# A decoder block's first stage: two shift/scale columns made earlier, output weights cut between the attention pairs, two heads of a pair interleaved

## The chip, the cores and the metric

The kernel runs on one core of one Trainium2 chip. The time is device microseconds from launch to end; before the change it is 1597.16 us, the median of three runs (1595.16 to 1599.23). A profiled execution of the same program took 1595.99 us; the span in its trace, from the first to the last instruction, is 1594.3 us.

## The reference, cut to what matters

One token block of 512 rows and 1024 columns goes through two sub-layers. The change is in the first: six vectors are made from the condition `c`, the rows are modulated, projected, sent through two kinds of attention, and the result is normalised per group and multiplied by an output matrix.

```python
ada = einsum('bd,de->be', silu(c), w_ada) + b_ada
shift1, scale1, gate1, shift2, scale2, gate2 = split(ada, 6)
h = x * (1.0 + scale1) + shift1
qa, ka, va, qb, kb, vb = split(h @ w_in)
# oa: 8 heads of 64 in a window of 128 keys, distance bias and a sink logit
#   (two key heads; query head j and j+4 share the pair number j)
scores = q @ k / sqrt(64) + bias           # blocks of 128 queries x 256 keys
m = max(max(scores), sink);  p = exp(scores - m)
oa = (p / (sum(p) + exp(sink - m))) @ va
# ob: 8 heads of 64, stick-breaking weights over all earlier keys
ob = stick_breaking(qb, kb, vb)
mix = concat(rms_norm(oa), rms_norm(ob)) @ w_out
x = layer_norm(ALPHA * x + gate1 * mix)
h = x * (1.0 + scale2) + shift2            # into the second sub-layer (PEER)
```

shift2 and scale2 are columns 3 and 4 of the six; gate1 is number 2. They are first needed when the first sub-layer is done.

## The kernel before, in words

The program is one core's work on five engines. TensorE (PE) multiplies, VectorE (DVE), ScalarE (ACT) and GpSimd (POOL) do the rest, SyncE (SP) issues the transfers. Each engine works off its list in order. In the first stage these lists are set by a scheduler that goes through the program text in its order, prefers parts marked `tc.high_priority()`, and fills in others as it thinks their inputs will be ready; tiles with the same tag share a ring of `bufs` buffers, and a step that needs a buffer waits for its last user. The later stages are written in a manual order and are not touched.

The first stage: the modulated rows are kept transposed, as a high and a low part (`hhi`, `hlo`). A projection chunk (`proj_chunk`, L303) loads 512 KB of weights into `uraw`, cuts them into `uhi` (ScalarE, L92) and `ulo` (VectorE, L93) and runs 24 matmuls of 512 columns into `pj`. `uraw`, `uhi` and `ulo` have two buffers each.

Stick-breaking works on pairs of heads j = 0 to 3. `sb_weights` takes the two heads one after the other through one score tile `z` (one buffer): scores `z<-q,k` (L367); ScalarE takes Abs, Exp and Ln into `e` (L370 to L372); VectorE makes the logarithms (L374); GpSimd masks them (L340, L342); two small VectorE steps (L376, L377); the cut into `sphi` (ScalarE) and `splo` (VectorE, L93); matmuls that add up the logarithms (L382, L384, first with `sphi`, then with `splo`); Exp into `e` (L387), masked again. `e` has two buffers, so the next pair's first head waits until `sb_values` (L398, `oacc<-e,vr`) has read the last pair's. Both functions are high priority.

Windowed attention works on pairs too (`swa_pair`, four of them). `swa_head` makes one head: eight score matmuls in the trace for one head (L421, `zs`, 64 of the 128 rows of the array, as each fp32 matmul is two records), a maximum with bias and sink (L424), exponentials (L431), the sum and the scaling by it (L436). Then `swa_pair` transposes the weights (`pt`, L451), copies them (L453, `pts`) and multiplies with the values (L456, `oacc`). `zs` and `pt` share the tag `s` with two PSUM banks; `oacc` of both kinds of attention is one bank.

The columns of shift2 and scale2 come from `ada_cols`: 4 MB of weights, eight VectorE steps into `acc` (L170, L172), eight matmuls with one column each (L179, `adap`), and one small addition (L181). The text has `ada_cols(3)` behind the projection chunks 6 and 7, and `ada_cols(4)` behind `sb_values` of pair 2. The output weights are eight slices: `load_wo` loads one into the same ring `uraw`, multiplies by gate1 (L502) and cuts it (`wohi`, `wolo`). Six of them follow the last projection chunk in the text, and the pair `swa_pair(3)` follows them. The output matmuls are `zm` (L556); the group norms need `ssp` (L521), a sum over all heads' squares.

```python
        w = sb(2, q0, k0)
        swa_pair(0, qa, ka)
        qa1 = proj_chunk(10, "qa")
        swa_pair(1, qa1, ka)
        q0, k0 = proj_chunk(6, "q"), proj_chunk(7, "k")
        ada_cols(3)
        sbv(2, w)
        ada_cols(4)
        w = sb(3, q0, k0)
```

Of the kernel before, what the change touches and what calls it, by code (L numbers as in the profile page):

```python
# [8 lines left out]
F32 = mybir.dt.float32  # L9
F32R = mybir.dt.float32r  # L10
# [4 lines left out]
AF = mybir.ActivationFunctionType  # L15
OP = mybir.AluOpType
# [16 lines left out]
NEG = -1e30  # L33
# [34 lines left out]
def tile_block(ctx, tc, xr, xT, ccol, wada, bcol, brow, wqk, wv, sinks, gncol, wout,  # L68
               ln1c, ln1r, wq, keys, u_rows, uT, v_rows, ln2r, out):
    nc = tc.nc  # L70
    V, A, G, T = nc.vector, nc.scalar, nc.gpsimd, nc.tensor
# [4 lines left out]
    wsp = ctx.enter_context(tc.tile_pool(name="wsp", bufs=2))  # L76
    small = ctx.enter_context(tc.tile_pool(name="small", bufs=2))
# [9 lines left out]
                    base=0, channel_multiplier=-1)  # L87
# [54 lines left out]
    with ExitStack() as front:  # L142
        fc = front.enter_context(tc.tile_pool(name="fc", bufs=1, side="right", reuse_waits="tile"))
        fa_cm = tc.tile_pool(name="fa", bufs=2, side="right")
        fa = fa_cm.__enter__()
        fw_cm = tc.tile_pool(name="fw", bufs=2)
        fw = fw_cm.__enter__()
        ps = front.enter_context(tc.tile_pool(name="psf", bufs=2, space=PSUM))
# [51 lines left out]
        part = fc.tile([P, 1], F32, name="part")  # L200
# [93 lines left out]
        def proj_chunk(i, nm):  # L294
            if i < 4:
                half_proj(i, len(PARTS) - 1)
                p = heads[i][1]
            else:
                hi, lo = load_w_in(i)
                p = ps.tile([P, S], F32, name="pj", tag="m", bufs=2)  # L300
                for dc in range(DC):
                    for n, (a, b) in enumerate(((hi, hhi), (hi, hlo), (lo, hhi))):
                        T.matmul(p, a[:, dc], b[:, dc], start=(dc == 0 and n == 0), stop=(dc == DC - 1 and n == 2))  # L303
            o = fw.tile([P, S], F32, name=nm, tag=nm)
            A.activation(o, p, AF.Copy, scale=0.125 if nm[0] == "q" else 1.0)
            return o

        vr = fw.tile([P, TB, 640], F32, name="vr", bufs=1)

        def proj_v(*halves):  # L310
            for half in halves:
# [5 lines left out]
                for tb in range(TB):  # L317
                    p = ps.tile([P, S], F32, name="pj", tag="m", bufs=2)
                    t = slice(tb * P, (tb + 1) * P)
                    for dc in range(DC):  # L320
# [11 lines left out]
                        base=0, channel_multiplier=1)  # L332
# [74 lines left out]
        def swa_head(j, r, qt, kt):  # L407
            h = j + 4 * r
            rs = slice(r * HD, (r + 1) * HD)
            prs = fw.tile([P, TB, 2 * P], F32, name="prs", bufs=3)  # L410
            nm, den, es = (small.tile([P, TB], F32, name=n, bufs=3) for n in ("nm", "den", "es"))
            bias = fw.tile([P, 2 * P], F32, name="bias")
            V.tensor_scalar(bias, dist, -(2.0 ** (-(h + 1.0))), None, op0=OP.mult)
            for keep_op, base, cm, st in ((OP.is_ge, P, 1, -1), (OP.is_gt, 0, -1, 1)):
                G.affine_select(out=bias, in_=bias, pattern=[[st, 2 * P]], compare_op=keep_op, fill=NEG,
                                base=base, channel_multiplier=cm)
            k0 = [P if qb == 0 else 0 for qb in range(TB)]
            for qh in range(2):
                z = ps.tile([P, 2, 2 * P], F32, name="zs", tag="s")
                for qb in (2 * qh, 2 * qh + 1):  # L420
                    T.matmul(z[:, qb % 2, k0[qb]:], qt[rs, qb * P:(qb + 1) * P],  # L421
                             kt[rs, (qb - 1) * P + k0[qb]:(qb + 1) * P], start=True, stop=True, skip_group_check=True)
                for qb in (2 * qh, 2 * qh + 1):
                    V.tensor_tensor_reduce(out=prs[:, qb, k0[qb]:], in0=z[:, qb % 2, k0[qb]:], in1=bias[:, k0[qb]:],  # L424
                                           scale=1.0, scalar=sink[:, h:h + 1], op0=OP.add, op1=OP.max,
                                           accum_out=nm[:, qb:qb + 1])
            V.tensor_scalar(nm, nm, -1.0, None, op0=OP.mult)
            V.tensor_scalar(es, nm, sink[:, h:h + 1], None, op0=OP.add)
            A.activation(es, es, AF.Exp)
            for qb in range(TB):  # L430
                A.activation(prs[:, qb, k0[qb]:], prs[:, qb, k0[qb]:], AF.Exp, bias=nm[:, qb:qb + 1],  # L431
                             accum_out=den[:, qb:qb + 1])
            V.tensor_tensor(den, den, es, op=OP.add)
            V.reciprocal(den, den)
            for qb in range(TB):
                V.tensor_scalar(prs[:, qb, k0[qb]:], prs[:, qb, k0[qb]:], den[:, qb:qb + 1], None, op0=OP.mult)  # L436
            return prs

        def swa_pair(j, qt, kt):
            prs = [swa_head(j, r, qt, kt) for r in range(2)]  # L440
            o = ps.tile([P, S], F32, name="oacc", tag="o", bufs=1)
            blocks = [(qb, kb) for qb in range(TB) for kb in ((qb - 1, qb) if qb else (qb,))]
            for n0 in (0, 4):
                part = blocks[n0:n0 + 4]
                w = len(part) * P
                pts = []
                for r in range(2):
                    pt = ps.tile([P, 512], F32, name="pt", tag="s")
# [48 lines left out]
        wo = [None] * DC

        def load_wo(c, pool):
            raw = wsp.tile([P, D], F32, name="uraw", tag="uraw")  # L500
            nc.sync.dma_start(raw, wout[c])
            V.tensor_tensor(raw, raw, gate1, op=OP.mult)  # L502
            wo[c] = (pool.tile([P, D], F32R, name=f"wohi{c}"), pool.tile([P, D], F32R, name=f"wolo{c}"))
            split(raw, *wo[c])

        ORDER = (4, 5, 6, 7, 0, 1, 2, 3)
# [670 lines left out]
```

## Time and profile before

| | |
|---|---|
| time, median of three runs | 1597.16 us |
| profiled execution, time and span | 1595.99 us, 1594.3 us |
| TensorE busy | 1554.9 us, 98% of the span |
| VectorE, ScalarE, GpSimd busy | 77%, 41%, 29% |
[...]
| the attention part of the first stage | about 58 to 257 us of the span |

[...] A timeline row gives the start in us from the span's start, how long the run of instructions took, engine, source line, operation, output and inputs, shape and count; in brackets how long the engine sat idle before it and what released it. A run that has no bracket began as soon as the one before it was done. The busy time of a pipelined TensorE contains overlap, so 98% does not mean that it works at its peak. The share of the whole span says little about one stage: the change is worth what it does between about 130 and 270 us.

### The profile page before, as it was taken

What the parts mean: (1) busy time and instruction counts of PE and PEld (TensorE: products, weight loads), DVE (VectorE), ACT (ScalarE), POOL (GpSimd) and SP (SyncE); (2) the same over time, 40 slices, a digit from 0 to 9 for tenths busy, and PEclk for the clock granted to TensorE, in tenths of its full rate; (3) what the DMA queues carried; (4) which work ended last, traced back from release to release, by engine and by line L of the source; (5) the groups of instructions that cost most, each with busy time, mean ns of one, the idle gap of its engine ahead of it and who ended that gap; (6) DMA issues with size and microseconds to landing.
All of it is one profiled execution on the core that took longest, in us unless ns stands there. A gap on an engine that the chain in (4) does not pass through costs nothing.

```text
span 1594.3 us, 21985 instructions
## 1 busy us (share of the span) xinstructions
PE 1554.9 (98%) x8109; PEld 1346.3 (84%) x8109; DVE 1220.3 (77%) x2351; ACT 647.5 (41%) x935; POOL 455.8 (29%) x410
## 2 busy tenths in 40 slices
PE   8999999999989999999999999999999999999996
PEld 5776767788879999899999999999999999998885
DVE  2568585589999997578777787777877777777878
ACT  2535574333355555333333333333333333333331
POOL 0002133544400000233334333333333444333100
PEclk8999898999999999999999999999999999999999
DMA  9564132222225555999888988999889998989873
GB/s 338 184 258 158 53 112 101 79 92 81 81 80 212 219 210 202 334 327 326 305 311 301 326 301 304 306 309 322 302 303 312 307 321 301 311 282 305 261 231 119
DMA packets 147356, 382.12 MB, mean 240 GB/s; under 512 B 11312, under 2 KB 68656, under 8 KB 143280
## 3 DMA queue, kind: packets, MB, share of 16 engines
q1 hardware_dynamic: 110384, 246.49, 44.6%
q0 software_dynamic: 36864, 134.23, 24.4%
q8 instruction: 63, 1.03, 0.3%
q14 instruction: 45, 0.37, 0.1%
HBM read 351.32 MB, written 29.36 MB: 239 GB/s over the span
## 4 chain that ended last, share of the span: by engine, by line
PE 79%; DVE 12%; DMA 3%; ACT 3%; issue 1%; POOL 1%; SPq 0%; DVEq 0%; ACTq 0%; POOLq 0%
PE yb L980 32%; PE ph L970 25%; PE pw L841 5%; PE ph L806 4%; PE pj L303 3%; PE zm L556 2%; DVE scr L620 1%; PE pj L274 1%; DMA wa<-in_wada_dram 1%; DVE tsi L622 1%; DVE tsi L619 1%; PE pq L647 1%; DVE tsv L621 1%; DVE tsv L618 1%; PE oacc L398 1%
## 5 line engine op out<-in xcount | busy, mean ns | idle before, releaser
L855 POOL DMA_INDIRECT gat<-in_u_rows_dram,idx x128 | 161.6, 1262 | 478.5 <-DVE hd L873 226.5
L93 DVE TENSOR_TENSOR ulo<-uraw,uhi 128x1024 fp32r<-128x1024 f32 x133 | 162.5, 1223 | 164.9 <-ACT uhi L92 160.5
L970 PE MATMUL ph<-h2hi,ulo 128*128 128x384 f32 x768 | 258.6, 337 | 0.6 <-DVE ulo L93 0.6
L970 PE MATMUL ph<-h2hi,uhi 128*128 128x384 f32 x768 | 258.2, 336 | 0.3 <-ACT uhi L92 0.3
L970 PE MATMUL ph<-h2lo,uhi 128*128 128x384 f32 x768 | 258.2, 336 | 0.0
L855 POOL DMA_INDIRECT gat<-in_v_rows_dram,idx x128 | 161.0, 1258 | 264.8 <-DVE y L883 224.1
L980 PE MATMUL yb<-vhi,ghi 128*128 128x512 f32 x654 | 203.0, 391 | 0.0
L980 PE MATMUL yb<-vhi,glo 128*128 128x512 f32 x654 | 202.9, 391 | 0.0
L980 PE MATMUL yb<-vlo,ghi 128*128 128x512 f32 x654 | 202.6, 391 | 0.0
L92 ACT ACTIVATE uhi<-uraw 128x1024 fp32r<-128x1024 f32 x155 | 162.4, 1050 | 74.6 <-PE pq L647 52.9
L883 DVE SCALAR_TENSOR_TENSOR y<-gat,cf,y 128x1024 f32<-128x1024 f32 x127 | 162.7, 1281 | 3.9 <-DMA gat<-in_v_rows_dram,idx 1.6
L873 DVE CUSTOM_DVE_ANT_0 gscr<-gat,h2row 128x1024 f32<-128x1024 f32 x128 | 156.5, 1222 | 10.6 <-DMA gat<-in_u_rows_dram,idx 7.9
L1085 ACT ACTIVATE stash<-ph 128x384 f32<-128x384 f32 x96 | 47.2, 491 | 275.1 <-PE ph L970 275.1
L970 PEld LDWEIGHTS ph<-h2lo,uhi 128*128 128x128 f32 x768 | 144.4, 188 | 4.4
L970 PEld LDWEIGHTS ph<-h2hi,uhi 128*128 128x128 f32 x768 | 144.4, 188 | 4.4 <-ACT uhi L92 0.7
L980 PEld LDWEIGHTS yb<-vlo,ghi 128*128 128x128 f32 x654 | 122.7, 188 | 27.3
L980 PEld LDWEIGHTS yb<-vhi,glo 128*128 128x128 f32 x654 | 122.8, 188 | 26.8
L970 PEld LDWEIGHTS ph<-h2hi,ulo 128*128 128x128 f32 x768 | 144.4, 188 | 1.0 <-DVE ulo L93 1.0
L980 PEld LDWEIGHTS yb<-vhi,ghi 128*128 128x128 f32 x654 | 121.8, 188 | 18.9
L93 DVE TENSOR_TENSOR vlo<-vraw,vhi 128x1024 fp32r<-128x1024 f32 x97 | 118.4, 1220 | 17.5 <-ACT vhi L92 17.4
L92 ACT ACTIVATE vhi<-vraw 128x1024 fp32r<-128x1024 f32 x97 | 102.8, 1060 | 53.6 <-issue 35.8
L947 ACT ACTIVATE ghi<-gt 128x384 fp32r<-128x384 f32 x97 | 51.0, 525 | 177.7 <-DVE gt L920 177.7
(311 smaller groups left out, 2860.1 us busy)
## 6 DMA issues: line engine op xcount, KB each, us to landing
uraw<-in_uT_dram SPq DMA_DIRECT2D x128, 512.0 KB, 5.2
vraw<-in_v_rows_dram SPq DMA_DIRECT2D x128, 512.0 KB, 5.2
w_d<-stage SPq DMA_DIRECT2D x12, 2048.0 KB, 7.3
wt<-w_d SPq DMA_DIRECT2D x32, 768.0 KB, 9.3
wa<-in_wada_dram SPq DMA_DIRECT2D x16, 1024.0 KB, 6.5
wah<-in_wada_dram SPq DMA_DIRECT2D x16, 512.0 KB, 9.4
uraw<-in_wq_dram SPq DMA_DIRECT2D x16, 512.0 KB, 3.3
uraw<-in_wqk_dram SPq DMA_DIRECT2D x11, 512.0 KB, 7.8
```

The costliest lines, as they stand in the source:

```text
L92: A.activation(hi, src, AF.Copy)
L93: (eng or V).tensor_tensor(lo, src, hi.bitcast(F32), op=OP.subtract)
L303: T.matmul(p, a[:, dc], b[:, dc], start=(dc == 0 and n == 0), stop=(dc == DC - 1 and n == 2))
L806: T.matmul(p[:, :ND], a[:, dc], b[:, dc, P:], start=(dc == 0 and n == 0), stop=(dc == DC - 1 and n == 2))
L841: T.matmul(p[:, k * P:(k + 1) * P], oh4[:, 1, :, k], oh4[:, 2 + j, :, k], start=(j == 0), stop=(j == 1), skip_group_check=True)
L855: G.indirect_dma_start(out=t, out_offset=None, in_=rows, in_offset=bass.IndirectOffsetOnAxis(ap=idx[:, k:k + 1], axis=0))
L873: V.tensor_tensor_reduce(out=scr, in0=t, in1=h2row, scale=1.0, scalar=0.0, op0=OP.mult, op1=OP.add, accum_out=hd[:, n:n + 1])
L883: V.scalar_tensor_tensor(y0, t, cf[:, k:k + 1], y0, op0=OP.mult, op1=OP.add)
L947: A.activation(gop[i][0], gts[i], AF.Copy)
L970: T.matmul(p[:, :ND], a[:, dc], b[:, dc, P:], start=(dc == 0 and n == 0), stop=(dc == DC - 1 and n == 2))
L980: T.matmul(ybank[b][c0 // 512][:, c0 % 512:(c1 - 1) % 512 + 1], x[:, t], y[:, c0:c1], start=(i == 0 and n == 0), stop=(n == 2 and i == (NK ...
L1085: A.activation(stash[i + LOOK], p[:, :ND], AF.Gelu_apprx_tanh)
```

## The change

Three edits in the first stage. `ada_cols(3)` and `ada_cols(4)`, and with them the release of the memory that their weights used, move ahead of `sb(2, ...)`. The six `load_wo` calls are spread over the text between the pairs. `swa_head` becomes `swa_scores`, which issues the score matmuls of both heads of a pair in turn, two score tiles at a time. In `swa_pair` the value matmuls are ordered by key block, so that two neighbouring query blocks go in one matmul of 256 columns: 8 for a pair where there were 14.

```diff
+        def swa_scores(j, qt, kt):
...
             for qh in range(2):
-                z = ps.tile([P, 2, 2 * P], F32, name="zs", tag="s")
+                zs = [ps.tile([P, 2, 2 * P], F32, name="zs", tag="s") for _ in range(2)]
                 for qb in (2 * qh, 2 * qh + 1):
-                    T.matmul(z[:, qb % 2, k0[qb]:], qt[rs, qb * P:(qb + 1) * P],
+                    for r in range(2):
+                        rs = slice(r * HD, (r + 1) * HD)
+                        T.matmul(zs[r][:, qb % 2, k0[qb]:], qt[rs, qb * P:(qb + 1) * P],
...
-            blocks = [(qb, kb) for qb in range(TB) for kb in ((qb - 1, qb) if qb else (qb,))]
+            blocks = [(qb, kb) for kb in range(TB) for qb in (kb, kb + 1) if qb < TB]
...
-                for n, (qb, kb) in enumerate(part):
+                for n in range(0, len(part), 2):
+                    qb, kb = part[n]
+                    c = min(2 * P, w - n * P)
...
         ka = proj_chunk(8, "ka")
+        ada_cols(3)
+        ada_cols(4)
+        fa_cm.__exit__(None, None, None)
+        fwo = front.enter_context(tc.tile_pool(name="fwo", bufs=1, side="right", reuse_waits="tile"))
         w = sb(2, q0, k0)
         swa_pair(0, qa, ka)
         qa1 = proj_chunk(10, "qa")
+        load_wo(ORDER[0], fwo)
         swa_pair(1, qa1, ka)
         q0, k0 = proj_chunk(6, "q"), proj_chunk(7, "k")
-        ada_cols(3)
+        load_wo(ORDER[1], fwo)
+        load_wo(ORDER[2], fwo)
         sbv(2, w)
-        ada_cols(4)
         w = sb(3, q0, k0)
...
         qa2 = proj_chunk(11, "qa")
+        load_wo(ORDER[3], fwo)
+        load_wo(ORDER[4], fwo)
+        load_wo(ORDER[5], fwo)
         swa_pair(2, qa2, ka)
         sbv(3, w)
         qa3 = proj_chunk(12, "qa")
...
-        for c in ORDER[:6]:
-            load_wo(c, fwo)
         swa_pair(3, qa3, ka)
```

Because a scheduler sets the lists, the text alone does not tell what stands where. Three places matter. The lines of the changed kernel are numbered anew: L421, L424, L436, L502 and L556 of before are L424, L430, L446, L488 and L573.

TensorE behind the last matmul of chunk 8 (`ka`), before; `zs` are the first pair's scores, `pj` is chunk 10, `z<-sphi` and `z<-splo` belong to the second head of stick-breaking pair 1:

```order
L421 MATMUL zs<-ka,qa 128x128
L421 MATMUL zs<-ka,qa 128x256 x3
L303 MATMUL pj<-hhi,ulo 128x512
L303 MATMUL pj<-hhi,uhi 128x512
L303 MATMUL pj<-hlo,uhi 128x512
L303 MATMUL pj<-hhi,ulo 128x512
L382 MATMUL z<-sphi,negtri 128x512 x2
L382 MATMUL z<-sphi,negtri 128x256
```

and now, from the same place to the second run of `adap`:

```order
L179 MATMUL adap<-ones,acc 128x1 x8
L424 MATMUL zs<-ka,qa 128x128 x2
L424 MATMUL zs<-ka,qa 128x256 x2
L382 MATMUL z<-sphi,negtri 128x512 x2
...
L382 MATMUL z<-splo,negtri 128x512 x2
L382 MATMUL z<-splo,negtri 128x256
L384 MATMUL z<-splo,negone 128x384
L384 MATMUL z<-splo,negone 128x256 x2
L384 MATMUL z<-splo,negone 128x128
L179 MATMUL adap<-ones,acc 128x1 x8
L303 MATMUL pj<-hhi,uhi 128x512
L303 MATMUL pj<-hlo,uhi 128x512
```

Both runs of `adap` stand here now, and the matmuls of chunk 10 stand behind the second of them.

VectorE at the same place, before, from the logarithms of that head (`e<-z,e`) to the low part `splo`:

```order
L374 SCALAR_TENSOR_TENSOR e<-z,e 128x1280
L93 TENSOR_TENSOR ulo<-uraw,uhi 128x1024
L376 COPY e<-e 128x128
L377 TENSOR_TENSOR e<-e 128x128
L93 TENSOR_TENSOR ulo<-uraw,uhi 128x1024
L424 ISA prs,nm<-zs,bias,sink 128x128
L424 ISA nm 128x1
L424 ISA prs,nm<-zs,bias,sink 128x256
L424 ISA nm 128x1
L93 TENSOR_TENSOR splo<-e,sphi 128x1536
```

and now:

```order
L374 SCALAR_TENSOR_TENSOR e<-z,e 128x1280
L181 TENSOR_TENSOR adac<-adap,bc 128x8
L172 SCALAR_TENSOR_TENSOR acc<-wa,silu,acc 128x1024
L376 COPY e<-e 128x128
L377 TENSOR_TENSOR e<-e 128x128
L172 SCALAR_TENSOR_TENSOR acc<-wa,silu,acc 128x1024
L430 ISA prs,nm<-zs,bias,sink 128x128
L430 ISA nm 128x1
L172 SCALAR_TENSOR_TENSOR acc<-wa,silu,acc 128x1024
L93 TENSOR_TENSOR splo<-e,sphi 128x1536
L172 SCALAR_TENSOR_TENSOR acc<-wa,silu,acc 128x1024
```

Four steps of `acc` and the addition that reads `adap` have come in, around `splo`; the two cuts of `ulo` have gone elsewhere.

VectorE where the weights of windowed pair 1 are scaled (`prs<-prs,den`, first one head, then the other), before:

```order
L434 RECIPROCAL den<-den 128x4
L436 TENSOR_SCALAR prs<-prs,den 128x128
L436 TENSOR_SCALAR prs<-prs,den 128x256 x3
L93 TENSOR_TENSOR splo<-e,sphi 128x1536
L433 TENSOR_TENSOR den<-den,es 128x4
L434 RECIPROCAL den<-den 128x4
L436 TENSOR_SCALAR prs<-prs,den 128x128
L436 TENSOR_SCALAR prs<-prs,den 128x256 x3
```

and now:

```order
L93 TENSOR_TENSOR splo<-e,sphi 128x1536
L443 TENSOR_TENSOR den<-den,es 128x4
L488 TENSOR_TENSOR uraw<-uraw,gate_374 128x1024
L444 RECIPROCAL den<-den 128x4
L443 TENSOR_TENSOR den<-den,es 128x4
L488 TENSOR_TENSOR uraw<-uraw,gate_374 128x1024
L446 TENSOR_SCALAR prs<-prs,den 128x128
L446 TENSOR_SCALAR prs<-prs,den 128x256 x3
L444 RECIPROCAL den<-den 128x4
L93 TENSOR_TENSOR wolo_1557<-uraw,wohi_1556 128x1024
L446 TENSOR_SCALAR prs<-prs,den 128x128
L446 TENSOR_SCALAR prs<-prs,den 128x256 x3
```

Three steps on output weights stand between the sum of the first head and the scaling of the second, and the first head is scaled behind `splo`.

## Rows read from the trace of the kernel before

**Rows 1.** Busy time by stretch: window in us, busy us and count by engine, granted clock, DMA.
```profile
136.00:146.00 10.00, 9.07 (x42) 6.52 (x41) 9.59 (x27) 5.53 (x12) 4.00 (x6) 1.00 0.33 105
146.00:187.00 41.00, 40.67 (x220) 28.92 (x219) 27.01 (x66) 28.29 (x55) 8.85 (x16) 1.00 0.12 37
187.00:200.00 13.00, 13.00 (x51) 9.33 (x51) 3.78 (x4) 4.04 (x6) 1.27 (x1) 0.50 0.15 49
...
238.00:241.00 3.00, 3.00 (x12) 1.62 (x9) 3.00 (x14) 0.57 (x3) 0.00 (x0) 0.50 1.00 401
...
255.00:262.00 7.00, 6.90 (x20) 4.94 (x20) 4.83 (x13) 5.35 (x9) 0.00 (x0) 0.51 0.33 92
```

**Rows 2.** Timeline of VectorE, 130 to 142 us.
```profile
130.01 2.61 DVE L172 SCALAR_TENSOR_TENSOR acc<-wa,silu,acc 128x1024 f32<-128x1024 f32 x2
134.60 1.49 DVE L374 SCALAR_TENSOR_TENSOR e<-z,e 128x1280 f32<-128x1280 f32 x1 [1.98 <-ACT e L372]
136.01 1.22 DVE L93 TENSOR_TENSOR ulo<-uraw,uhi 128x1024 fp32r<-128x1024 f32 x1
...
137.88 0.29 DVE L377 TENSOR_TENSOR e<-e 128x128 f32<-128x128 f32 x1
...
139.22 0.34 DVE L424 CUSTOM_DVE_ANT_0 prs<-zs,bias,sink 128x128 f32<-128x128 f32 x1
...
139.90 1.75 DVE L93 TENSOR_TENSOR splo<-e,sphi 128x1536 fp32r<-128x1536 f32 x1
```

**Rows 3.** Timeline of TensorE, 137 to 147 us.
```profile
137.19 1.78 PE L421 MATMUL zs<-ka,qa 64*128 64x128 f32 x8 [0.93 <-ACT ka L305]
...
142.28 0.75 PE L382 MATMUL z<-splo,negtri 128*128 128x512 f32 x3
...
145.62 1.77 PE L367 MATMUL z<-q,k 64*128 64x512 f32 x4
```

**Rows 4.** Timeline of TensorE at 169 us: two heads in one run.
```profile
169.35 1.13 PE L421 MATMUL zs<-ka,qa 64*128 64x256 f32 x8
```

**Rows 5.** The chain that ended last, 180 to 202 us: start, us, what.
```profile
181.77 0.78 PE pt L451 x7
...
182.78 1.68 PE adap L179 x16
184.46 0.59 PE oacc L456 x8
...
189.81 3.20 PE adap L179 x16
...
199.33 2.83 PE oacc L398 x16
```

**Rows 6.** Timeline of VectorE: the second head of windowed pair 1.
```profile
180.19 1.07 DVE L436 TENSOR_SCALAR prs<-prs,den 128x128 f32<-128x128 f32 x4
```

**Rows 7.** Timeline of ScalarE, 182 to 198 us.
```profile
182.94 0.59 ACT L453 ACTIVATE pts<-pt 128x512 f32<-128x512 f32 x1
...
196.51 0.69 ACT L349 ACTIVATE oT<-oacc,gn 128x512 f32<-128x512 f32 x1 [5.17 <-PE oacc L456]
197.09 0.59 ACT L355 ACTIVATE sq<-oacc 128x512 f32<-128x512 f32 x1
```

**Rows 8.** Timeline of VectorE, stick-breaking pair 3, second head.
```profile
223.73 1.21 DVE L502 TENSOR_TENSOR uraw<-uraw,gate 128x1024 f32<-128x1024 f32 x1
224.86 1.48 DVE L374 SCALAR_TENSOR_TENSOR e<-z,e 128x1280 f32<-128x1280 f32 x1
```

**Rows 9.** Timeline of GpSimd, the same head's last mask.
```profile
232.84 2.96 POOL L93 TENSOR_TENSOR hlo<-oT,hhi 128x512 fp32r<-128x512 f32 x2
235.75 1.58 POOL L340 TENSOR_SCALAR_AFFINE_SELECT e<-e 128x384 f32<-128x384 f32 x1
```

**Rows 10.** Timeline of TensorE: the value matmuls behind it.
```profile
237.38 4.05 PE L398 MATMUL oacc<-e,vr 128*64 128x512 f32 x14 [1.68 <-POOL e L340]
```

**Rows 11.** Transfers of the output weights: count, KB each, median us to landing.
```profile
uraw<-in_wout_dram SPq DMA_DIRECT2D x8, 512.0 KB, 3.4
```

More of the change, by code (lines that the diff above doesn't have):

```diff
@@ L405, in tile_block @@
         G.iota(dist, pattern=[[-1, 2 * P]], base=P, channel_multiplier=1, allow_small_or_imprecise_dtypes=True)
[L407 to L416, printed above, removed]
+        def swa_scores(j, qt, kt):
+            prs = [fw.tile([P, TB, 2 * P], F32, name="prs", bufs=3) for _ in range(2)]
+            nms, biases = [], []
+            for r in range(2):
+                nms.append(small.tile([P, TB], F32, name="nm", bufs=3))
+                bias = fw.tile([P, 2 * P], F32, name="bias")
+                V.tensor_scalar(bias, dist, -(2.0 ** (-(j + 4 * r + 1.0))), None, op0=OP.mult)
+                for keep_op, base, cm, st in ((OP.is_ge, P, 1, -1), (OP.is_gt, 0, -1, 1)):
+                    G.affine_select(out=bias, in_=bias, pattern=[[st, 2 * P]], compare_op=keep_op, fill=NEG,
+                                    base=base, channel_multiplier=cm)
+                biases.append(bias)
@@ L423, in swa_head @@
[L423 to L436, printed above, removed]
+                    for r in range(2):
+                        rs = slice(r * HD, (r + 1) * HD)
+                        T.matmul(zs[r][:, qb % 2, k0[qb]:], qt[rs, qb * P:(qb + 1) * P],
+                                 kt[rs, (qb - 1) * P + k0[qb]:(qb + 1) * P], start=True, stop=True,
+                                 skip_group_check=True)
@@ new lines, in swa_scores @@
+                for r in range(2):
+                    h = j + 4 * r
+                    for qb in (2 * qh, 2 * qh + 1):
+                        V.tensor_tensor_reduce(out=prs[r][:, qb, k0[qb]:], in0=zs[r][:, qb % 2, k0[qb]:],
+                                               in1=biases[r][:, k0[qb]:], scale=1.0, scalar=sink[:, h:h + 1],
+                                               op0=OP.add, op1=OP.max, accum_out=nms[r][:, qb:qb + 1])
+            for r in range(2):
+                h = j + 4 * r
+                nm = nms[r]
+                den, es = (small.tile([P, TB], F32, name=n, bufs=3) for n in ("den", "es"))
+                V.tensor_scalar(nm, nm, -1.0, None, op0=OP.mult)
+                V.tensor_scalar(es, nm, sink[:, h:h + 1], None, op0=OP.add)
+                A.activation(es, es, AF.Exp)
+                for qb in range(TB):
+                    A.activation(prs[r][:, qb, k0[qb]:], prs[r][:, qb, k0[qb]:], AF.Exp, bias=nm[:, qb:qb + 1],
+                                 accum_out=den[:, qb:qb + 1])
+                V.tensor_tensor(den, den, es, op=OP.add)
+                V.reciprocal(den, den)
+                for qb in range(TB):
+                    V.tensor_scalar(prs[r][:, qb, k0[qb]:], prs[r][:, qb, k0[qb]:], den[:, qb:qb + 1], None,
+                                    op0=OP.mult)
@@ L437, in swa_head @@
             return prs
         def swa_pair(j, qt, kt):
-            prs = [swa_head(j, r, qt, kt) for r in range(2)]
+            prs = swa_scores(j, qt, kt)
             o = ps.tile([P, S], F32, name="oacc", tag="o", bufs=1)
-            blocks = [(qb, kb) for qb in range(TB) for kb in ((qb - 1, qb) if qb else (qb,))]
+            blocks = [(qb, kb) for kb in range(TB) for qb in (kb, kb + 1) if qb < TB]
             for n0 in (0, 4):
@@ L453, in swa_pair @@
                     A.activation(pts[r][:, :w], pt[:, :w], AF.Copy)
-                for n, (qb, kb) in enumerate(part):
+                for n in range(0, len(part), 2):
+                    qb, kb = part[n]
+                    c = min(2 * P, w - n * P)
                     for r in range(2):
-                        T.matmul(o[r * HD:(r + 1) * HD, qb * P:(qb + 1) * P], vr[:, kb, r * HD:(r + 1) * HD],
-                                 pts[r][:, n * P:(n + 1) * P], start=(n == 0 and n0 == 0), stop=(n0 == 4 and n == 2),
+                        T.matmul(o[r * HD:(r + 1) * HD, qb * P:qb * P + c], vr[:, kb, r * HD:(r + 1) * HD],
+                                 pts[r][:, n * P:n * P + c], start=(n == 0 and n0 == 0), stop=(n0 == 4 and n == 2),
                                  skip_group_check=True)
@@ L468, in sbv, with load_wo @@
                 sb_values(j, w)
+        wo = [None] * DC
+        def load_wo(c, pool):
+            raw = wsp.tile([P, D], F32, name="uraw", tag="uraw")
+            nc.sync.dma_start(raw, wout[c])
+            V.tensor_tensor(raw, raw, gate1, op=OP.mult)
+            wo[c] = (pool.tile([P, D], F32R, name=f"wohi{c}"), pool.tile([P, D], F32R, name=f"wolo{c}"))
+            split(raw, *wo[c])
+        ORDER = (4, 5, 6, 7, 0, 1, 2, 3)
         w = sb(0, proj_chunk(0, "q"), proj_chunk(1, "k"))
@@ L496, in tile_block @@
         qa3 = proj_chunk(12, "qa")
[L497 to L506, printed above, removed]
-        for c in ORDER[:6]:
-            load_wo(c, fwo)
         swa_pair(3, qa3, ka)
```

3 lines of the change are left out of this document (removed).

## The prediction

> **What bounds the kernel now.** The busy table by stretch comes first [rows 1]. [...]
>
> Next the chain that ended last, around the first such stretch [rows 5]. It runs through the two `adap` runs of 16 records, 1.68 us at full clock and 3.20 us at half, and ends at the value matmuls of stick-breaking pair 2 (L398), at 199.33, 2.83 us long, done at 202.16. That is the hinge: the next pair's first head has to wait for them, since they read its buffer `e`. Whatever makes L398 earlier moves all that follows. Before it stand, one behind the other, the scaled weights of windowed pair 1, done at 181.26 [rows 6], their transposes, copies and value matmuls [rows 5, 7], and the bank of `oacc` that both kinds of attention share. What comes after is read from timelines [rows 8 to 10].
>
> **Place A: the columns made early (136 to 150 us).** VectorE, step by step. Before, two steps of `acc` end at 132.62 and VectorE then idles 1.98 us [rows 2]. The new list has one more of them here (about 1.3 us each, 2.61 for two [rows 2]) and the cut `ulo` (1.22) ahead of `e` (1.49): 132.62 + 1.3 + 1.2 + 1.5 = 136.6, against 136.1 before. Now the addition L181 waits for the first `adap` run. TensorE ended chunk 8 at 136.26 (137.19 less 0.93 [rows 3]); 1.68 us more is 137.9, so VectorE goes on at 138.1. One `acc` step, 139.4; L376 and L377, 140.0 (before 138.17); a step, 141.3; a maximum of 0.34 with its read-out, 141.7; a step, 143.0; `splo`, 1.75, done at 144.75 against 141.65. Its matmuls on TensorE take about 1.2 us [rows 3], 145.95; the last `acc` step ends at 146.05, and only then can the second `adap` run start, to 147.75. Behind it in TensorE's queue stand two matmuls of chunk 10 and four records of scores; the like took 2.1 us before, now 1.8. So `z<-q,k` of stick-breaking pair 2 starts at 149.55, not 145.62: **+3.9 us**. The eight VectorE steps and the two `adap` runs are not dearer than before; what costs is that chunk 10, which filled TensorE here, is queued behind them. [...]
>
> **From there to the hinge.** Between `z<-q,k` and the scaled weights of pair 1 VectorE gets output-weight work. Four such steps stand in the way of pair 1's second head: a cut before it, two multiplications by gate1 and one cut among its own steps. At 1.21 to 1.22 us [rows 2, 8] that is 4.9 us. I add 1.3 us for the maxima of the other head, which now stand before a head's own sum (0.34 us and more each [rows 2]; bounds 0 and 2.6). So these weights are ready at 181.26 + 3.9 + 4.9 + 1.3 = 191.4. From there before took until 199.33, 18 us, because two `adap` runs lay between and the clock fell. Without both I add up one pass: transposes 0.78, copy 0.59, value matmuls 0.59, the same three again for the second half, then 0.69 and 0.59 on ScalarE [rows 5, 7]: 5.2 us. L398 starts at 196.6. It took 4.05 us at half clock [rows 10], so 2.0 at full, and ends at 198.6 against 202.16: **-3.5 us**. The merged value matmuls (8 for 14) and the scores done in turn take TensorE work away; here it is hidden beside the chain, and I count nothing for it. If TensorE is what is late, it counts (a rival below).
>
> **From the hinge to the output matmuls.** With most output weights cut already, three waits shrink. The logarithms L374 of pair 3's second head no longer stand behind a multiplication by gate1 (1.21, and L374 starts as it ends [rows 8]): 1.0. GpSimd's last mask stood directly behind two cuts `hlo` of 2.96 together [rows 9], which the new list has earlier; TensorE idled 1.68 us for it [rows 10]: 0.9, between 0 and 1.68. With the shorter idle L398 of pair 3 may miss the low clock: 4.05 becomes 2.0 [rows 10]. Against it: the last scores of windowed pair 3's second head now stand behind L398 in TensorE's queue, half a run of 1.13 [rows 4] and two maxima, 1.3. Net **-2.6 us**, bounds -4.6 and +1.3.
>
> **The clock.** Between 136.3 and 149.6 TensorE now has scores (1.1), two sets of `z` matmuls (2.4), two `adap` runs (3.4) and the 1.8 above, the rest, 4.6 us, is idle. Before, it was busy 9.07 of 10 us here and had 1.00 [rows 1]. `adap` takes one column per matmul, and the long fall came right after such a run [rows 1, 5]. So I expect that the low stretch moves to here rather than going away. One of 7 us, as at 255 [rows 1], costs half: **+3.4 us**; bounds 0, and 6.5 for one as long as 187 to 200.
>
> **Sum.** -3.5 - 2.6 + 3.4 = -2.7. The profiled execution took 1595.99 us, so 1593.3; the median of the runs is 1.17 above it, so 1594.5 us.
>
> **Rivals.**
> - The clock stays up at place A, because the scores of two heads and the `z` matmuls keep TensorE active enough. For it: the first `adap` run of before, 182.78 to 184.46, lies in a stretch at 1.00 [rows 1, 5]. Against it: two such runs and 4.6 us of idle within 13 us. 1594.5 - 3.4 = 1591.1.
> - TensorE's own work is the bound. For it: 53.67 of 54 us busy before the hinge [rows 1]. A run of eight score records of one head took 1.78 us [rows 3], one with both heads in it 1.13 [rows 4], so 0.65 less; four pairs with two runs each give 5.2, of which pair 1 had 0.65 before: 4.5 us less work. Against it: chunk matmuls lie around as filler and the chain is what L398 waits for. 1594.5 - 4.5 = 1590.0. [...]
> - Slower. The output weights share the ring `uraw` with the chunks. In the new list the multiplications for slices 4 to 6 come one or two steps behind the cut that frees their buffer, but a transfer takes 3.4 us to land [rows 11]. VectorE works in order, so pair 1's scaling, the last chunk's cut and the logarithms of stick-breaking pair 3 wait behind. Three such waits are 10.2 us: 1604.7. It decides from about 7.5 us on, if those waits fall before the hinge and not into VectorE's idle time, of which there was 9.2 us from 187 to 200 [rows 1]. That idle time speaks against it.
> - The change does not do what it says: in the list the second halves of windowed pair 0 stand apart, one head each, so nothing overlaps there. I gave that nothing in the sum, so the time stays.
>
> **How the numbers follow.** 0.3%, 4.8 us, is about what a measurement of this kernel can tell from no change: below 1592.4 is faster, above 1602.0 slower. Forecast 0.44 (with 0.02 beyond each bound), clock stays 0.19, TensorE bound 0.18, slower 0.19. So faster 0.39, same 0.40, slower 0.21. The forecast's own range is 1591 to 1600. For 8 in 10 I take 1588.5 (the second rival with 1.5 us less of the low clock) to 1603.0, which leaves out most of the slow case.
>
> **What would show it.** Right, step by step: `z<-q,k` of pair 2 starts near 149.6; a stretch at 0.50 begins between 138 and 150 and none lies at 187; pair 1's second head is scaled near 191 with L488 steps in front; L398 of pair 2 ends near 198.6 plus what the clock costs; L398 of pair 3 takes near 2 us. Wrong: clock 1.00 from 136 to 155; idle VectorE released by a transfer of the output weights; or an end of the stage that does not follow L398.

## The result, and the profile after

The changed kernel takes 1603.39 us (median of 20 runs), the kernel before 1596.3 in the same comparison: a ratio of 1.0056, 95% interval 1.0044 to 1.0068 (all runs go into it; the two medians alone give 1.0044). It is slower, by more than the 0.3% named in the prediction; the forecast was 1594.5 us. The profiled execution has a span of 1600.8 us against 1594.3.

The busy table of after, over the stretches that answer to [rows 1] (window, busy us and count of PE, PEld, DVE, ACT, POOL, granted TensorE clock as a share of full speed, DMA share, GB/s):

```profile
136.00:146.00 10.00, 6.42 (x40) 5.54 (x38) 8.11 (x13) 3.03 (x3) 0.77 (x2) 0.79 0.17 53
146.00:162.00 16.00, 16.00 (x42) 8.80 (x42) 5.55 (x15) 3.28 (x6) 1.56 (x4) 0.50 0.21 66
162.00:187.00 25.00, 25.00 (x127) 18.09 (x125) 16.59 (x42) 20.74 (x35) 4.66 (x7) 1.00 0.13 43
187.00:200.00 13.00, 12.45 (x59) 9.30 (x58) 12.85 (x30) 10.49 (x26) 6.67 (x8) 1.00 0.27 88
...
230.50:237.40 6.90, 5.81 (x19) 4.02 (x21) 5.26 (x10) 2.98 (x5) 2.00 (x3) 0.51 0.00 0
...
255.00:262.00 7.00, 6.45 (x41) 4.50 (x39) 1.35 (x1) 2.68 (x5) 1.28 (x1) 1.00 0.00 0
```

The low stretch at 187 us is gone, as forecast, and so is the one at 255. In their place stand one of 20.5 us (141.8 to 162.3; 0.79 is its first part) and one of 6.8 us at 230.5. VectorE, 9.2 us idle from 187 to 200 before, is now busy for 12.85 of 13 us.

The chain of after, which answers to [rows 3, 5] (start, us, what):

```profile
136.01 1.69 PE adap L179 x16
...
142.08 1.68 DVE splo L93
143.76 0.04 issue
143.81 1.44 PE z L382 x3
145.24 0.85 PE z L384 x4
146.10 3.31 PE adap L179 x16
149.41 1.06 PE pj L303 x2
150.47 2.00 PE zs L424 x4
152.47 2.99 PE z L367 x4
...
190.73 4.19 DMA uraw<-in_wout_dram
194.92 0.02 issue
194.95 1.28 DVE uraw L488
...
205.94 2.35 PE oacc L398 x16
208.29 1.22 ACT e L370
```

The second `adap` run takes 3.31 us, twice the first; `z<-q,k` of pair 2 follows at 152.47, where 149.55 was forecast. A transfer of the output weights stands in the chain for 4.19 us, which the third rival named (what it cost is taken up with e7). L398 of pair 2, the hinge, ends at 208.29; before, 202.16.

To compare kernels I cut each one's timeline at the same instructions, since the part ahead of the change shifts by some 3 us from one profiled execution to another: from the first `z<-q,k` of stick-breaking pair 1 (125.44 before, 126.14 after) to that of pair 2 (part A), to the end of L398 of pair 2 (B, up to the hinge), to the first `ssp` matmul (C). "Low" is the time at a granted clock of 0.50 from 100 us to the `zt` transposes, in steps of 0.5 us. The ratios are to runs of before taken along with each kernel's own, with their 95% intervals. A, B, C and low come from one profiled execution each, and some of these lie off their kernel's median: e3 4.1, e5 3.1 and e12 3.4 us below it, e8 2.1, e9 1.9 and e13 6.5 us above. From the first `ssp` to the end of the span e5 takes 1338.6 us and e13 1344.4, so the parts don't add up to the differences of the times.

| kernel | us | ratio | A | B | C | low |
|---|---|---|---|---|---|---|
| before | 1596.3 | 1 | 20.18 | 56.54 | 51.46 | 24.5 |
| after | 1603.39 | 1.0056 (1.0044–1.0068) | 26.13 | 55.97 | 51.83 | 27.5 |
| e1 interleave alone | 1600.66 | 1.0014 (0.9999–1.0029) | 19.60 | 57.52 | 55.63 | 27.5 |
| e2 columns early alone | 1608.04 | 1.0061 (1.0044–1.0079) | 26.57 | 59.68 | 51.07 | 27.5 |
| e3 no interleave | 1609.38 | 1.0077 (1.0063–1.0091) | 27.04 | 57.20 | 53.08 | 34 |
| e4 chunk 10 ahead | 1613.38 | 1.0097 (1.0078–1.0115) | 28.52 | 55.04 | 61.02 | 45 |
| e5 wide columns, after | 1602.99 | 1.0038 (1.0023–1.0052) | 24.84 | 58.43 | 51.73 | 27.5 |
| e6 wide columns, before | 1591.31 | 0.9958 (0.9943–0.9972) | 20.13 | 49.12 | 50.17 | 3.5 |
| e7 own ring | 1616.54 | 1.0113 (1.0096–1.0130) | 26.60 | 56.87 | 53.68 | 41 |
| e8 weights late | 1603.73 | 1.0038 (1.0024–1.0053) | 26.42 | 53.95 | 54.68 | 30 |
| e9 wide + chunk 10 | 1593.78 | 0.9984 (0.9969–0.9999) | 21.87 | 54.00 | 48.37 | 7 |
| e10 wide + interleave | 1594.53 | 0.9983 (0.9973–0.9993) | 19.60 | 49.82 | 57.00 | 13.5 |
| e11 wide + filler | 1605.39 | 1.0057 (1.0038–1.0076) | 21.49 | 52.54 | 63.16 | 27.5 |
| e12 e9, weights late | 1597.74 | 1.0008 (0.9997–1.0019) | 21.89 | 51.00 | 55.66 | 13 |
| e13 e9, no interleave | 1591.40 | 0.9968 (0.9949–0.9987) | 21.44 | 53.64 | 50.51 | 13.5 |

### The profile page after: what moved, and what is told of

Read it like the earlier page. It is cut to its first block, busy times and chain, and to the rows that moved or that the text cites. A ratio compares the mean times of both kernels' runs of the same rounds, so it can differ in the third digit from the quotient of the medians.

```text
span 1600.8 us, 21885 instructions
## 1 busy us (share of the span) xinstructions
PE 1553.5 (97%) x8061; PEld 1342.3 (84%) x8061; DVE 1220.4 (76%) x2351; ACT 647.9 (40%) x935; POOL 455.9 (28%) x410
## 4 chain that ended last, share of the span: by engine, by line
PE 79%; DVE 13%; ACT 3%; DMA 3%; issue 1%; POOL 0%; SPq 0%; DVEq 0%; ACTq 0%
PE yb L997 32%; PE ph L987 25%; PE pw L858 5%; PE ph L823 4%; PE pj L303 2%; PE zm L573 2%; DVE scr L637 1%; DMA wa<-in_wada_dram 1%; PE pj L274 1%; DVE tsi L639 1%; DVE tsi L636 1%; PE z L367 1%; PE pq L664 1%; DVE acc L172 1%; DVE tsv L638 1%
## 5 line engine op out<-in xcount | busy, mean ns | idle before, releaser
L997 PEld LDWEIGHTS yb<-vlo,ghi 128*128 128x128 f32 x654 | 122.7, 188 | 27.3
```

What stands on the lines that cost most here:

```text
L997: T.matmul(ybank[b][c0 // 512][:, c0 % 512:(c1 - 1) % 512 + 1], x[:, t], y[:, c0:c1], start=(i == 0 and n == 0), stop=(n == 2 and i == (NK ...
```

## The experiments

Three theories were open after the two traces. Clock: the early columns empty TensorE at place A, and the slow stretch there costs the time. Output weights: their steps and transfers in front of pair 1's scaling cost it. Interleaving: the two heads of a windowed pair get into each other's way.

**One part of the change at a time (e1, e2, e3).**

```diff
 e1, on before: swa_head and swa_pair replaced by those of the change
-            prs = [swa_head(j, r, qt, kt) for r in range(2)]
+            prs = swa_scores(j, qt, kt)
 e2, on before:
         ka = proj_chunk(8, "ka")
+        ada_cols(3)
+        ada_cols(4)
...
-        ada_cols(3)
         sbv(2, w)
-        ada_cols(4)
 e3, on after: swa_scores and swa_pair replaced by those of before
```

e1: 

> Before with the windowed pairs of the change alone: both heads interleaved, merged value matmuls; the columns ada_cols(3) and (4) and the output weights stay where before had them. Clock theory (the loss comes from the emptied TensorE behind the early columns): not slower than before, 1592 to 1597 us, the long stretch at 0.50 stays at 187 to 200 us. Output-weight theory (multiplications that wait for their transfer in front of pair 1's scaling): the same, 1592 to 1597. Interleaving theory (a head's own sum stands behind the other head's maxima, and the banks of two heads block each other): about 1600, with pair 1's second head scaled some us later than 181.3.

e2: 

> Before with ada_cols(3) and ada_cols(4) behind chunk 8, nothing else. Clock theory: the granted clock falls to 0.50 near 142 us for 15 us or more as in after, z<-q,k of pair 2 starts near 152 in place of 145.6, the stretch at 187 to 200 goes; about 1600 us, if the later gain of the removed columns (some 3.5 us) does not pay for it, 1597. Output-weight theory: no new wait, so 1592 to 1596. Interleaving theory: 1592 to 1596.

e3: 

> After with the windowed pairs of before (one head behind the other); columns early and output weights between the pairs stay. Clock theory: the stretch at 0.50 from 142 us stays, 1601 to 1605 us. Output-weight theory: 1601 to 1605 as well, with the multiplication L.. by gate1 waiting for uraw in front of the scaling. Interleaving theory: back to 1595 to 1598.

The early columns alone (e2) are as slow as the whole change: 1.0061 to 1.0056, with a fall at the same place (140.5 to 168 us) and part A 26.57. So they are enough for the loss. Interleaving alone (e1) makes 1.0014, which can't be told from no change, and taking it out (e3) doesn't bring the time back to the 1595 to 1598 us of its theory. It is not the main cause. The clock theory has the order of the three right, but its times were too low: 1592 to 1597, about 1600 and 1601 to 1605 us were expected, 1600.66, 1608.04 and 1609.38 came. The spread output weights alone, on before, were not run.

**What makes the clock fall at place A (e4, e5, e6, e9).** In before, in after and in e1 to e3 the fall came behind the first run of one-column `adap` matmuls; in after TensorE also had idle time there, 2.45 and 1.12 us:

```profile
140.99 0.85 PE L382 MATMUL z<-sphi,negtri 128*128 128x512 f32 x3 [2.45 <-ACT sphi L92]
143.81 1.44 PE L382 MATMUL z<-splo,negtri 128*128 128x512 f32 x3 [1.12 <-DVE splo L93]
```

These four runs separate the two.

```diff
 e4, on after:
         ka = proj_chunk(8, "ka")
+        qa1 = proj_chunk(10, "qa")
         ada_cols(3)
...
-        qa1 = proj_chunk(10, "qa")
 e5, on after, and e6, on before (ada_cols):
-                T.matmul(p[:, dc:dc + 1], acc[:, dc * P:(dc + 1) * P], ones[:, 0:1], start=True, stop=True,
+                T.matmul(p[:, dc * 64:(dc + 1) * 64], acc[:, dc * P:(dc + 1) * P], ones[:, 0:64], start=True, stop=True,
...
-            V.tensor_tensor(adac[:, g * 8:g * 8 + 8], p[:, :DC], bc[:, g * 8:g * 8 + 8], op=OP.add)
+            V.tensor_tensor(adac[:, g * 8:g * 8 + 8], p.rearrange("p (c n) -> p c n", c=DC)[:, :, 0], bc[:, g * 8:g * 8 + 8], op=OP.add)
 e9, on after: both
```

e4: 

> After with chunk 10 made directly behind chunk 8, ahead of the two early columns, so that TensorE has 6 us of dense work for the time in which the columns' accumulation runs on VectorE. Clock theory: the fall at 142 us is gone or short, z<-q,k of pair 2 no later than 152.5, 1595 to 1599 us. Output-weight theory: the waits of 4.2 us in front of pair 1's scaling stay, 1602 to 1604. Interleaving theory: 1602 to 1604.

e5: 

> After with each of the 32 adap matmuls of the two early columns 64 columns wide in place of one (64 columns of ones, the first of each eight kept); the same weights are loaded. Narrow-columns theory (the clock falls because of the run of one-column matmuls, since it fell 2.4 to 5.7 us behind the first such run in before, after and e1 to e4, and in e4 with TensorE busy 10.00 of 10 us): no fall at 142 us, or one of at most 7 us, z<-q,k of pair 2 near 150 in place of 152.5, 1592 to 1598 us. Idle theory (it falls because TensorE stands idle 2.85 and 1.31 us behind the run): the fall of 20.5 us stays, 1602 to 1605 us.

e6: 

> Before with the same 32 adap matmuls 64 columns wide, at their late place. Narrow-columns theory: the stretch at 0.50 from 187 to 200 us goes, L398 of pair 2 ends some 4 to 6 us earlier than 202.16, 1589 to 1593 us: faster than before. Idle theory: it stays, 1595 to 1598 us.

e9: 

> After with both edits of e4 and e5: the 32 adap matmuls 64 columns wide, and chunk 10 ahead of the early columns. Both theories taken together (a one-column run without idle time was enough for the fall in e4, idle time with a wide run was enough in e5): neither is left, so no fall at 142 us, z<-q,k of pair 2 near 149, L398 of pair 2 ends near 200 in place of 206.9 in e4; since chunk 10 then lacks later on, 1597 to 1606 us, at least 7 us below e4's 1613.4. If something else makes the clock fall there (the half-height score and z matmuls): the fall stays, 1608 to 1614 us.

Busy tables around place A, columns as above. First e4 (one-column run, TensorE filled):

```profile
134.00:142.00 8.00, 8.00 (x48) 6.94 (x46) 5.99 (x7) 3.32 (x4) 1.69 (x2) 1.00 0.16 58
142.00:150.00 8.00, 8.00 (x32) 6.37 (x33) 3.79 (x11) 1.67 (x2) 0.76 (x2) 0.56 0.00 0
150.00:162.00 12.00, 12.00 (x25) 5.26 (x25) 3.78 (x11) 1.71 (x6) 1.85 (x2) 0.50 0.30 89
```

e5 (wide run, TensorE idle behind it):

```profile
134.00:142.00 8.00, 5.09 (x35) 4.17 (x34) 6.72 (x11) 3.04 (x3) 0.77 (x2) 0.93 0.23 87
142.00:150.00 8.00, 7.22 (x26) 6.50 (x27) 4.48 (x11) 1.39 (x2) 0.77 (x2) 0.50 0.00 0
```

e9 (wide run, TensorE filled):

```profile
134.00:142.00 8.00, 8.00 (x38) 6.59 (x37) 7.55 (x9) 4.08 (x4) 1.69 (x2) 1.00 0.39 151
142.00:150.00 8.00, 8.00 (x53) 6.27 (x51) 6.00 (x7) 2.78 (x3) 1.01 (x2) 1.00 0.23 68
150.00:162.00 12.00, 12.00 (x57) 8.00 (x56) 7.58 (x27) 8.10 (x12) 3.04 (x6) 1.00 0.13 43
```

In e4 TensorE has no idle time in the records from 134 to 162 us, and the clock falls all the same, to 0.50 at 143 us. In e5 the run is wide and the clock falls to 0.50 where TensorE was busy 5.09 of 8 us and waited 2.46 and 1.22 us. Of these only e9, with both removed, stays at 1.00. So my two theories were each half right: here either a one-column run or the idle time was enough. e9 alone would not show it, because its list differs from e4's in more than the width: the score matmuls that stand between the two `adap` runs in e4 stand behind them in e9. That these matmuls, whose rows show a form of `64*128` or `128*64` in place of `128*128`, make the clock fall by themselves is ruled out by e9: from 147.46 to 154.50 us it runs only scores, `z<-q,k` and value matmuls, at 1.00. e4 was the dearest miss: its expectation of 1595 to 1599 rested on idle time alone and 1613.38 came.

e6 shows the other side: in before TensorE was busy around the late columns [rows 1], and there the wide run was enough. From 146 to 190 us of before both kernels have the same matmuls in the same order, so here the width is the only difference up to the fall (186.7 us). The timeline of e6, and its busy table where before had 0.50 [rows 1, 5]:

```profile
183.21 1.89 PE L179 MATMUL adap<-ones,acc 128*128 128x64 f32 x16
...
190.95 1.33 PE L179 MATMUL adap<-ones,acc 128*128 128x64 f32 x10
...
192.96 2.37 PE L398 MATMUL oacc<-e,vr 128*64 128x512 f32 x16
```

```profile
187.00:200.00 13.00, 13.00 (x82) 9.53 (x81) 5.81 (x6) 8.68 (x12) 2.38 (x2) 1.00 0.27 99
```

TensorE is busy for 13.00 us in both kernels, but gets 82 matmuls done in place of 51. The hinge ends at 195.33, not 202.16, and the time is 0.9958 of before: the lowest median of this study, with one edit of two lines (e13, at 0.9968, can't be told from it).

One more run of one-column matmuls stands in all kernels: `ssp`, 16 records. The last low stretch of e6, from 249.7 us, comes behind it, and so does the one at 255 in before (`ssp` at 253.62). In e6:

```profile
245.50 1.95 PE L521 MATMUL ssp<-ones,sqa 128*128 128x1 f32 x16 [0.57 <-POOL sqa L356]
```

In after the same run (260.07) has no fall behind it, so such a run is not always followed by one. A wider `ssp` was not tried.

**Idle time removed by work of no use (e11).**

```diff
 on e5, in ada_cols(4), ahead of its wide run:
+            for _ in range(20):
+                T.matmul(p[:, :P], ones, ones, start=True, stop=True, skip_group_check=True)
```

> e5 with 20 matmuls of ones by ones (128 columns, into the columns' own bank, overwritten by the second wide run) in TensorE's list behind the first run, 17 of them where e5 has its 2.46 us of idle time. Clock theory: the fall from 141 to 161.5 us goes or shrinks to 7 us, z<-q,k of pair 2 near 148, L398 of pair 2 ends near 199 to 202 in place of 207.8, 1592 to 1597 us. Output-weight and queue theory (what is late is VectorE's list, not TensorE's clock): the clock stays up, but L398 of pair 2 ends after 205 all the same and the time is 1600 to 1604 us.

Half of it came as the clock theory said: 1.00 from 136 to 162 us, part A 21.49, and L398 of pair 2 ended at 197.31, 11 us earlier than in after. The busy row:

```profile
136.00:162.00 26.00, 25.81 (x145) 18.83 (x144) 18.00 (x42) 14.53 (x29) 5.55 (x9) 1.00 0.06 21
```

The total did not follow (1605.39): a fall of 13.5 us came at 204.5 us, in the part behind the hinge, and C became 63.16. Just ahead of it TensorE had stood idle for 1.26 and 0.96 us; that this made the clock fall was not tested. What was won ahead of the hinge was given back behind it. I did not try to remove that second fall.

**The output weights (e7, e8, e12).**

```diff
 e7, on after:
-            raw = wsp.tile([P, D], F32, name="uraw", tag="uraw")
+            raw = (fwo.tile([P, D], F32, name="wraw", bufs=2) if pool is fwo else
+                   wsp.tile([P, D], F32, name="uraw", tag="uraw"))
...
-        load_wo(ORDER[5], fwo)
...
-        for c in ORDER[6:]:
+        for c in ORDER[5:]:
 e8, on after, and e12, on e9: the six load_wo calls taken out, and
+        for c in ORDER[:6]:
+            load_wo(c, fwo)
         swa_pair(3, qa3, ka)
```

e7: 

> After with a ring of two buffers of their own for the output weights, in their pool (the sixth slice, for which the memory then does not do, is made with the last two). Output-weight theory: the wait of 4.2 us at 190.7 and those of 1.3 and 2.3 us behind it are gone, L398 of pair 2 ends 3 to 5 us before 208.3, 1598 to 1601 us. Clock theory: as the fall at 142 us stays, the time moves by less than 2 us from after's, 1601 to 1605 us.

e8: 

> After with the six output-weight slices back in front of windowed pair 3; columns early and heads interleaved. Clock theory: the fall from 142 to 162 us stays, 1600 to 1605 us. Output-weight theory: the multiplications no longer stand in front of pair 1's scaling, L398 of pair 2 ends near 202 in place of 208.3, 1595 to 1599 us.

e12: 

> e9 (wide adap matmuls, chunk 10 ahead of the early columns) with the six output-weight slices back in front of windowed pair 3. If the output-weight steps in front of pair 1's scaling cost what the step of the prediction says (4.9 us, on the chain to the hinge): L398 of pair 2 ends 49 to 50 us behind z<-q,k of pair 2 in place of 54.0, and the time from there to the last matmuls of the stage is some 2 to 3 us longer (e8 against after); 1590 to 1593 us. If these steps lie beside other work: 53 to 55 us as in e9, and 1594 to 1598 us, since only the later part is longer.

VectorE around pair 1's scaling (L446) in after, in e7 and in e8 (start, us, engine, line, operation):

```profile
191.25 1.87 DVE L93 TENSOR_TENSOR splo<-e,sphi 128x1536 fp32r<-128x1536 f32 x1
...
193.32 1.21 DVE L488 TENSOR_TENSOR uraw<-uraw,gate 128x1024 f32<-128x1024 f32 x1
...
194.95 1.28 DVE L488 TENSOR_TENSOR uraw<-uraw,gate 128x1024 f32<-128x1024 f32 x1
196.15 1.33 DVE L446 TENSOR_SCALAR prs<-prs,den 128x128 f32<-128x128 f32 x4
...
198.62 1.06 DVE L446 TENSOR_SCALAR prs<-prs,den 128x128 f32<-128x128 f32 x4
```

```profile
194.45 1.21 DVE L489 TENSOR_TENSOR wraw<-wraw,gate 128x1024 f32<-128x1024 f32 x1
195.86 1.44 DVE L446 TENSOR_SCALAR prs<-prs,den 128x128 f32<-128x128 f32 x4
198.68 1.10 DVE L446 TENSOR_SCALAR prs<-prs,den 128x128 f32<-128x128 f32 x4
```

```profile
188.17 1.08 DVE L446 TENSOR_SCALAR prs<-prs,den 128x128 f32<-128x128 f32 x4
191.69 1.07 DVE L446 TENSOR_SCALAR prs<-prs,den 128x128 f32<-128x128 f32 x4
```

With buffers of their own the transfers are no longer waited for there, yet the scaling ends at 199.78, 46.8 us behind `z<-q,k` of pair 2 (153.0); in after it is 47.4 (199.68 less 152.27). So the 4.19 us in the chain of after (190.73 to 194.92) were not what the wait cost: VectorE had other steps to do in that time, as its rows show. (e7's total is 13.2 us above after's, outside what either theory gave; 8.2 of it lie in the output part, where three slices are made in place of two and the 13 us from `ssp` to `zt` became 21.2.) Without the weight steps (e8) the scaling ends at 192.76, 7 us earlier, but the hinge only 2.2 us (206.09), and C is 2.9 us longer: the total is that of after. So the hinge doesn't follow the scaling one for one. With the clock up (e12 against e9, one execution each) the weights in front cost 3.0 us before the hinge and give 7.3 back behind it; the 51.0 us of e12's B lie between the two theories. By the medians the spreading gains 4.0 us; the intervals, 0.9969 to 0.9999 and 0.9997 to 1.0019, still overlap a little.

**Interleaving with the clock up (e10, e13).** The edits are e1's with e6's, and e9's with e3's.

e10: 

> e1 with the 32 adap matmuls 64 columns wide; columns and output weights late, as in before. Narrow-columns theory: the stretch at 0.50 from 184.5 to 198 us of e1 goes, its L398 of pair 2 ends near 194 to 196 in place of 200.9, 1590 to 1596 us. If interleaving is a gain of its own it comes below e6 (1591.3), if it is a loss (1.4 us were taken by e1 behind before, within what can be told) above it.

e13: 

> e9 (wide adap matmuls, chunk 10 ahead of the early columns, output weights between the pairs) with the windowed pairs of before, one head behind the other. If interleaving is a loss wherever the clock is up (e10 against e6: 57.0 against 50.2 us behind pair 2's value matmuls): some 3 to 6 us less than e9, 1588 to 1591 us, faster than e6. If it pays beside the early columns, as after against e3 says: 1596 to 1600 us, with the longer part ahead of pair 2's value matmuls. If it does nothing: within 2 us of e9's 1593.8.

The costliest groups behind the hinge (194 to 251 us), first of e10, then of e6 (line, operation, count, busy us, mean ns, idle time before and its releaser):

```profile
L469 PE MATMUL oacc<-pts,vr 128*64 128x256 f32 (+1 forms) x32 | 7.7, 450 | 3.4 <-ACT pts L464 3.3
L462 PE MATMUL pt<-ident,prs 128*128 128x128 f32 x28 | 7.0, 394 | 3.0 <-DVE prs L446 2.7
```

```profile
L456 PE MATMUL oacc<-pts,vr 128*64 128x128 f32 x56 | 5.6, 283 | 0.4 <-ACT pts L453 0.4
L451 PE MATMUL pt<-ident,prs 128*128 128x128 f32 x28 | 4.6, 282 | 0.0
```

Interleaved, TensorE waits 6.4 us in this stretch for the scaled and copied weights of a pair, 0.4 us without, and up to `zt` the clock falls three times (13.5 us) in place of once (3.5). C is 57.0 against 50.2; what the waits and what the falls add to it is not separated. e10 is slower than e6: 0.9983 (0.9973 to 0.9993) to 0.9958 (0.9943 to 0.9972), intervals that lie just apart. Beside the early columns e13 against e9 points the same way in the medians (1591.40 to 1593.78), and after against e3 the other way (1603.39 to 1609.38), but in both the intervals overlap; there it stays open.

## Why the prediction was wrong

Its profiled execution should have moved by -2.7 us; the span moved by +6.5. By its own steps:

- **Place A.** Right in its order: 136.01 for the first `adap` run, the addition L181 behind it, `splo` (end 143.76; I had 144.75), then the second run. Part A was to take 24.11 us and took 26.13. The working had left the clock at 1.00 there; half speed came instead, as in the run of 3.20 before [rows 5]: `splo`'s matmuls 2.29 us for some 1.2, the run 3.31 for 1.7, and the chunk matmuls and scores behind it 3.06 (1.06 and 2.00) for 1.8 are 4.0 us. With the clock up (e9, e11), A is 21.9 and 21.5, less than forecast.
- **The clock: the step that failed, by its size.** That the low stretch would move here was right. It was put at 7 us, after the one at 255 [rows 1], and at +3.4. It lasted 20.5 us, longer than the 13 us of 187 to 200 from which I took the upper bound, and a second one of 6.8 us came at 230.5. At half speed some 4.0 us are lost up to `z<-q,k` of pair 2, 5.0 from there to 162.3 (half of 10) and at most 3.4 behind the hinge: 12.4 in place of 3.4, an estimate. These 9.0 us are nearly all of the 9.2 by which the change of the span was missed; the other misses (A 2.0 us less, B 1.9 more, C 0.4 less, a start 0.7 us later) nearly cancel. I saw the columns' one-column matmuls as a suspect, and still priced the fall by the one at 255 and not by the longer one that stood behind an `adap` run. Ahead of that one TensorE had been busy 40.67 of 41 us [rows 1], and e6 shows that the width of the run decided there: with 64 columns the clock stays at 1.00 from 187 to 200 us. e11 and e9 bear the step out: A and B together took 82.10 us, forecast 73.16; with the clock held at place A they take 74.03 (filler) and 75.87 (wide run and chunk 10). That e9's time, 1593.78 us, is close to the forecast 1594.5 is partly luck, since its A is 2.2 us shorter and its B 5.0 us longer than forecast.
- **From there to the hinge.** 49.05 us forecast, 55.97 measured: 5.0 are the clock by the estimate above, 1.9 the rest. The four weight steps and the late scaling came nearly as worked out: 41.9 us from `z<-q,k` to the end of the scaling forecast, 47.4 measured, 42.4 without the 5.0. The way from there to L398, 18 us before and 5.2 in the forecast, took 6.3 (199.68 to 205.94), without the `adap` runs and at 1.00; e6, which removed only the low clock, shortened B by 7.4.
- **From the hinge to the output matmuls.** -2.6 forecast, +0.4 measured in C. L398 of pair 3 did go back to 2.38 us at full clock, and the last scores stood behind it; TensorE idled 0.24 us ahead of it where before had 1.68 [rows 10], and that the shorter wait is what kept the clock up was an estimate that no run tested. But TensorE waited 4.03 us for the copies of windowed pair 2's weights, and the new fall at 230.5, which begins as that wait ends and has no one-column run ahead of it, cost up to 3.4. In the timeline of TensorE in after:

```profile
230.56 1.11 PE L469 MATMUL oacc<-pts,vr 128*64 128x256 f32 x2 [4.03 <-ACT pts L464]
...
244.09 2.38 PE L398 MATMUL oacc<-e,vr 128*64 128x512 f32 x16 [0.24 <-issue]
246.39 1.13 PE L424 MATMUL zs<-ka,qa 64*128 64x256 f32 x4
```

- **The interleaving, counted at nothing.** It does take TensorE work away. The score groups of before and of e1, 125 to 262 us:

```profile
L421 PE MATMUL zs<-ka,qa 64*128 64x256 f32 (+1 forms) x64 | 14.7, 371 | 1.3 <-ACT ka L305 0.9 <-DVE nm L424 0.3
```

```profile
L424 PE MATMUL zs<-ka,qa 64*128 64x256 f32 (+1 forms) x64 | 11.4, 378 | 1.5 <-ACT ka L305 0.9 <-DVE nm L430 0.5
```

  That is 3.3 us less, of the 4.5 in the second rival. Still e1 was not faster, and the waits of e10 suggest where it went: both heads' weights come late together. So less work for TensorE did not make the kernel shorter, as the forecast said. With the wide columns of e6 a price of nothing was too kind, since e10 is 3.2 us above e6 by the medians.
- **The slower rival** got the direction and nearly the time (1604.7), but by luck, through another mechanism. Its transfers are there: 4.19 us in the chain, during which VectorE was not idle, and idle time of VectorE of 1.26 us at 202.08 and 2.25 at 211.39. e7 shows that waiting for them ahead of the scaling is not what decided.
- **The clock stays up** was wrong at place A. **The change does not do what it says** (pair 0's halves apart) was true in the list and made no difference that these runs show.

What stays open: why the fall at place A lasted 20.5 us in after and up to 27.3 in e2, why e11's part C is so much longer than e9's, and by how much the falls behind the hinge (204 to 265 us) decide between variants. They move with every edit.

## What to carry to other kernels

Before moving small steps to another place, see what TensorE has left to do there: a step taken off one wait can empty the engine at the new place, and here 20.5 us at half the clock followed. Price a fall by the longest similar stretch in the trace, and don't take even that as an upper bound: here the longest, at 187 us, was 13.7 us. Where a run of very narrow matmuls stands ahead of a low stretch, try it wider before rearranging anything: here 64 columns for one, in the kernel as it stood, took 0.4% off the time, where the rearrangement added 0.6%. That holds where nothing else empties TensorE: in the changed kernel the wide run alone (e5) left the fall in place, at 0.50 from 142 to 150 us with TensorE busy 5.09 of the 8 us ahead.

## What the runs showed of the hardware

- In after TensorE was busy 16.00 of 16 us from 146 to 162 and stayed at 0.50 throughout, with `adap`, `z<-q,k` and value matmuls; much the same `z<-q,k` and value matmuls ran at 1.00 in before (146 to 187, [rows 1]). So the stretch stayed at 0.50 although TensorE had no idle time in the records of these 16 us.
- The `adap` run of 16 records took 1.68 us with one column [rows 5]; with 64 columns the timeline row has 1.89 (e6), and 1.84 for one column (e4). By these timeline rows the width cost 0.05 us, and in e6 the low stretch of 13 us behind it was gone.
- Between 120 and 275 us of the fifteen traces, a fall with TensorE busy 10.00 of the 10 us ahead came only behind the one-column `adap` run: at 186.7 us in before, 184.6 in e1, 136.0 in e3 and 143.0 in e4.
